# Whole first loads and a re-joined instruction order in a one-core hybrid decoder layer

## The chip, the core and the metric

The kernel runs on one core of a Trainium2 chip. The core has a matrix engine (PE, with PEld for the loading of the stationary operand), a vector engine (DVE), an activation engine (ACT), a general engine (POOL, GpSimd) and a sync engine (SP) whose queue here issues nearly every DMA. Each engine works through its own list of instructions strictly in order; an instruction waits for semaphores of the instructions and transfers it depends on, and everything behind it on that engine waits with it.

The metric is the device time of one execution in microseconds (us); less is better.

## The reference

One decoder layer on a sequence of 512 tokens with 1024 features, batch 1, all in float32. The conditioning vector `c` gives six modulation vectors, the layer mixes tokens by a recurrent group and an attention group, and then runs a squared-ReLU MLP with 4096 hidden features. Cut to what matters here:

```
mod = silu(c) @ ada_w + ada_b
sh1, sc1, g1, sh2, sc2, g2 = split(mod, 6)
h = modulate(rms_norm(x, pre_norm_mix), sh1, sc1)      # h * (1 + sc1) + sh1
z = h @ w_in                                           # first projections
y = concat(rms_norm(gelu(g) * rg_lru(conv4(xr))), rms_norm(nsa_attention(q, k.., v.., gates))) @ w_out
x = x + (1 + g1) * rms_norm(y, post_norm_mix)
h = modulate(rms_norm(x, pre_norm_mlp), sh2, sc2)
y = square(relu(h @ w_ff1)) @ w_ff2                    # up projection, down projection
x = x + (1 + g2) * rms_norm(y, post_norm_mlp)
```

The output must match in float32, so each float32 operand of a large product is split into a high part (`hi`, a rounded form that the matrix engine takes at its fast rate) and a low part (`lo`, the rest), and a product is three matmuls: hi by h, lo by h, hi by the low part of h.

## The kernel before

**Stages.** Tokens lie in four tiles of 128. The kernel loads `x` (`xt[0..3]`, shown by the profile as `r`), sums the squares of each token (`norm_x`, line 864; scratch `att`, totals `stat`), scales `x` by the result, transposes it 128 columns at a time (`tp`), and applies the modulation (`h[j]` and its low part, `pt` being the float32 copy between). `j` runs over eight blocks of 128 features. The loop `first_wave` (line 917) does for each `j`: the modulation sums, the transposes, `h[j]`, the split of the weight tile `a{j}`, and 18 matmuls of 128x512 into six PSUM banks (`f`, `f`, `s`, `s`, `pv`, `pv`). After that come the other projections, the recurrence and the attention, the out projection, the residual, the up projection (`up_first`, `up`, with `up_pair` a seven-product form on tiles B and C made by adding and subtracting raw weight tiles), and the down projection (`down_all`, tiles D, d, e, s, also with fewer products). The end squares and sums the result per token tile and stores.

**Modulation sums.** `silb` is silu(c) spread over all partitions. It is made early: ACT and DVE form `sil`, eight matmuls against `ident` put it into two PSUM banks, and two copies (`silb[0:512]`, `silb[512:1024]`) bring it back. `ada_load` (line 880) loads rows of the modulation weights (`p<-in_ada_a`, two tiles of 128x1024 per `j`, one for the shift, one for the scale). `ada_sums(j)` (line 888) multiplies each tile by `silb` and adds along the row on DVE (`tensor_tensor_reduce`, CUSTOM_DVE_ANT_0 in the profile), giving `sa{j}`, which `h[j]` needs. For `j = 0` alone, tiles 0 and 1 are loaded as two halves each and summed as two halves each.

**Weights.** `Weights.load` (line 536) issues the loads of a tile, `Weights.split` (line 549) makes `hi` and `lo`. Tile `a0` (128x768) is loaded in three pieces of 256 columns and split in three pieces; `a1` to `a7` are loaded and split whole.

**The row of sums for the last gate.** While the up projection ends and the down projection begins, stream G2 (`ada_row`) loads 512 KB tiles `ar<-in_ada_r` and sums them on DVE, eight in turn; each load waits for the buffer of the sum before it.

**What sets the order.** The program first records every instruction as a node (`Clocks.put`, line 291). `flush` (line 283) then emits the nodes sorted by a number that stands for each node in `PLAN`, two characters of base 92 per node. Where an operation can run on more than one engine, the letter in `PLACE` for its stream picks the engine (`a` ACT, `d` DVE, `p` POOL); streams are named, for example `XN` (norm), `WS` (splits), `UP`, `DN` (up and down projection). So PLAN and PLACE together fix, for every engine and for the DMA queue, which instruction comes after which; nothing is decided while the kernel runs. The program has 5468 nodes.

Of the kernel before, what the change touches and what calls it, by code (L numbers as in the profile page):

```python
# [14 lines left out]
P = 128  # L15
S = 512
# [44 lines left out]
    '#0#1#5#=#6#>#8#:#9#2#7#a#H#I#J#K#[#L#M#N#O#Z#$#&###(#)#+#*#,#/#%#.#o#-#p$C#n#G#P#Q#R#S#z#{#|#}#~$#$$'  # L61
    '$%$&$($*$0$1#@#D#E#s#r$8#W#X#l#u#t$7#3#4#B#C#V#F$N#b#Y#k#m#q#v$L#c#e#d#f#h$A$E$)$-$.$/$4$5$6$>$B$D#x'
    '$<#T$:#w$;$H$X$`$U$V$^$_$[$b$i$W$g$e$h$c$j$d$k$f$?#j$@$G$F$+$,$2$3$J$K$R$9$P%4$}%$$y$v$w$|$~%)%#$x%&'
    '%+%;%<%,%%%(%.$S$=$O%2$I$Y$Z$]$a$l$m$p$M$T%8%F%=%@%9%:%C%q%?%B%A%E%K%s%y%D%O%G%N$Q$o$r%3%5$z${%*%-%/'
    '%0%T$n$s%m%t%z%L&&%u%p%w%{%M&(%v%r&/&#%~&*&4%x$t$q%V%7%6%P%Q%R%S%^%]%b%1%W%o&5&-&$&0&I%|&=&.&,&3&V%}'
    '&>&2&1&:&W&G%Y%X%[%>%H%I%J%a%`%e%_%c%n&?&7&;&B&_&Y&@&A&<&D&`&Z&^&X&C&E&b&[%Z%d%h&%&)&+&F&K&M&R&J&P(h'
    '&a&]&h&i&g&e&f(=&m&j&r&o&t(>&n&k&~&u%j%f%i&6&8&9&H&L&O&U&N&T(f&v(?&p&l(@&{&w(I&q&y(D&|&x(N&s&z(F&}#y'
    '(&(6(2(:(#($(((%()(*(u(t,i%k)X(v)^(}(-(3(4(<(5(9(p(|(;(7)*)))Z)i)V)h+&+((o(m+r*X)Y+$*0*1+o*Y&Q(+(0%l'
    '&S(,(1(g(x(l)g)}*V)$*W*#*`*%*a*&*b*v++*w+3*y+5*|+t*},8/i/@/C5U(8.%#A)U(k)S&d(/(A(B(C(j&c(.(i(n(w#;#<'
    '#U#]#^#_#`#g#i$u%U%g(E(G(H)#(r(z)%({*7*]*_*c+1+4-y(J(K(L/(#?/D/n0$(M(O(Q(V(Z([(](^(_(`(a(b(c(d(e*4(s'  # L70
    '(~)(*[+2.J/g(P(R(S(T(U(W(X(Y(q(y)&)+).)/)0)1)6)<)=)W)])|)>)?)@)A)B)C)D)I)T)j)~)J)K)L)N)O)P)Q)R)[)f)k'
    '*$)c)d)e),)-)2)3)4)5)7)8)9):);)E)F)G)H)M)_)`)a)b)l)m)n)o*/*-*5*z)r)s)t)u)v)w)x)y*.*6*x)z){*(*)***+*,'
# [1862 lines left out]
```

## Time and profile before

| what | us |
|---|---|
| median of 3 runs | 588.47 (588.38 to 588.47) |
| the profiled execution's own time | 588.5 |
| its span (first to last instruction) | 586.7 |
| granted TensorE clock, mean | 0.998 of full speed |

The page of the profile gives busy times per engine, a picture of the span in 40 slices, and a chain of work that ended last. The trace behind it answers views: windows (busy time of each engine in a stretch, with counts), the timeline (each instruction with start, duration, and in square brackets how long its engine stood idle before it and what ended that), waits, and the DMA issues. Durations overlap a little on an engine, since instructions are pipelined, so the distance between two starts is the better price where there is one. `L343` is the matmul helper, `L346` the transpose helper, `L353` the ACT helper, `L387` the DVE and POOL helper, `L443` the load: nearly all instructions carry one of these lines and are told apart by their tiles.

### The profile page before, as it was taken

What the parts mean: (1) busy time and instruction counts of PE and PEld (TensorE: products, weight loads), DVE (VectorE), ACT (ScalarE), POOL (GpSimd) and SP (SyncE); (2) the same over time, 40 slices, a digit from 0 to 9 for tenths busy, and PEclk for the clock granted to TensorE, in tenths of its full rate; (3) what the DMA queues carried; (4) which work ended last, traced back from release to release, by engine and by line L of the source; (5) the groups of instructions that cost most, each with busy time, mean ns of one, the idle gap of its engine ahead of it and who ended that gap; (6) DMA issues with size and microseconds to landing.
All of it is one profiled execution on the core that took longest, in us unless ns stands there. A gap on an engine that the chain in (4) does not pass through costs nothing.

```text
span 586.7 us, 9981 instructions
## 1 busy us (share of the span) xinstructions
PE 572.7 (98%) x3410; PEld 499.5 (85%) x3410; DVE 550.1 (94%) x1143; ACT 416.5 (71%) x849; POOL 227.2 (39%) x212
## 2 busy tenths in 40 slices
PE   6999999999999999999999999999999999999995
PEld 5688889878888898899999999998778888788884
DVE  5999999999999999999999999999999999998877
ACT  6658877999999999788747666574757676555314
POOL 4203323656847288651234242532101400114453
PEclk9999999999999999999999999999999999999999
DMA  8989895142242410022342423337343444344303
GB/s 314 417 314 344 295 396 220 59 142 73 94 177 91 151 65 1 19 91 73 109 147 106 139 77 108 110 120 273 129 154 121 157 140 151 122 144 155 132 1 144
DMA packets 27875, 89.12 MB, mean 152 GB/s; under 512 B 3360, under 2 KB 4272, under 8 KB 27824
## 3 DMA queue, kind: packets, MB, share of 16 engines
q1 hardware_dynamic: 27392, 88.27, 42.4%
q8 instruction: 27, 0.44, 0.3%
q10 hardware_dynamic: 432, 0.20, 0.1%
q14 instruction: 24, 0.20, 0.1%
HBM read 86.36 MB, written 2.11 MB: 151 GB/s over the span
## 4 chain that ended last, share of the span: by engine, by line
PE 86%; DVE 7%; issue 1%; ACT 1%; DMA 1%; POOL 0%; DVEq 0%; POOLq 0%
PE f L343 27%; PE pv L343 21%; PE s L343 20%; PE tp L343 14%; PE tp L346 4%; DVE r L387 2%; DVE p L387 2%; DMA ar<-in_ada_r 1%; DVE fT L387 0%; DVE lo_D L387 0%; ACT junk L353 0%; POOL stat L387 0%; DVE K L387 0%; DVE lo_q L387 0%; DVE h L387 0%
## 5 line engine op out<-in xcount | busy, mean ns | idle before, releaser
L387 POOL TENSOR_SCALAR p<-p,den 128x32 f32<-128x32 f32 (+4 forms) x48 | 46.3, 977 | 17.9 <-DVE den L387 10.4
L353 ACT ACTIVATE p<-p,mx 128x32 f32<-128x32 f32 (+4 forms) x96 | 45.2, 474 | 3.9 <-DVE mx L387 3.7
L343 PE MATMUL f<-hi_o,h 128*128 128x512 f32 x128 | 44.5, 406 | 0.0
L353 ACT ACTIVATE fT<-fT 128x512 f32<-128x512 f32 x50 | 29.5, 620 | 9.8 <-DVE fT L387 9.7
L346 PE MATMUL tp<-ident,p 128*128 128x128 f32 x192 | 36.3, 274 | 0.0
L343 PE MATMUL pv<-pt,V 128*128 128x256 f32 x160 | 36.3, 303 | 0.0
L343 PE MATMUL s<-K,Q 128*128 128x288 f32 (+4 forms) x128 | 36.1, 333 | 0.0
L387 DVE TENSOR_TENSOR pt<-tp,pt 128x512 fp32r<-128x512 f32 (+1 forms) x56 | 34.0, 607 | 2.0 <-ACT pt L353 0.5
L353 ACT ACTIVATE hi_B<-raw_A 128x512 fp32r<-128x512 f32 x32 | 20.1, 629 | 19.8 <-DVE raw_A L387 11.6
L387 DVE CUSTOM_DVE_ANT_0 p<-p,silb 128x1024 f32<-128x1024 f32 (+1 forms) x24 | 28.9, 1217 | 0.7 <-DMA p<-in_ada_a 0.7
L343 PEld LDWEIGHTS pv<-pt,V 128*128 128x128 f32 x160 | 26.7, 190 | 3.0 <-DVE pt L387 0.9
L346 PEld LDWEIGHTS tp<-ident,p 128*128 128x128 f32 x192 | 24.4, 141 | 4.8 <-issue 1.3
L343 PEld LDWEIGHTS f<-hi_o,h 128*128 128x128 f32 x128 | 23.5, 188 | 3.6 <-issue 0.3
L353 ACT ACTIVATE pt<-tp 128x512 fp32r<-128x512 f32 (+1 forms) x46 | 24.3, 534 | 3.0 <-PE pv L343 1.6
L353 ACT ACTIVATE junk<-r 128x1024 bf16<-128x1024 f32 (+2 forms) x17 | 13.7, 807 | 16.7 <-DVE r L387 16.2
L343 PEld LDWEIGHTS s<-K,Q 128*128 128x128 f32 x128 | 22.5, 188 | 3.3 <-PE f L343 0.4
L353 ACT ACTIVATE hi_D<-raw_d 128x1024 fp32r<-128x1024 f32 x14 | 14.8, 1060 | 14.1 <-DVE raw_d L387 9.7
L343 PE MATMUL f<-lo_o,h 128*128 128x512 f32 x64 | 24.8, 397 | 0.0
L353 ACT ACTIVATE hi_e<-raw_e 128x1024 fp32r<-128x1024 f32 x13 | 13.7, 1057 | 13.9 <-PE pv L343 5.0
L343 PE MATMUL f<-third,hi_B 128*128 128x256 f32 x96 | 23.4, 284 | 0.0
L387 POOL TENSOR_TENSOR fl<-fS,fh 128x256 fp32r<-128x256 f32 x3 | 6.5, 2176 | 42.6 <-ACT fh L353 42.6
L343 PE MATMUL tp<-r,hi_B 128*128 128x256 f32 x96 | 22.9, 283 | 0.0
(441 smaller groups left out, 2349.8 us busy)
## 6 DMA issues: line engine op xcount, KB each, us to landing
p<-in_ada_t SPq DMA_DIRECT2D x16, 512.0 KB, 7.0
ar<-in_ada_r SPq DMA_DIRECT2D x16, 512.0 KB, 4.3
p<-in_ada_a SPq DMA_DIRECT2D x14, 512.0 KB, 7.2
raw_d<-in_wd SPq DMA_DIRECT2D x14, 512.0 KB, 3.2
raw_e<-in_wd SPq DMA_DIRECT2D x14, 512.0 KB, 3.3
raw_A<-in_wf SPq DMA_DIRECT2D x12, 512.0 KB, 3.2
raw_B<-in_wf SPq DMA_DIRECT2D x12, 512.0 KB, 3.3
r<-in_x SPq DMA_DIRECT2D x8, 512.0 KB, 5.7
```

What stands on the lines that cost most here:

```text
L343: lambda: self.nc.tensor.matmul(out, lhs, rhs, start=start, stop=stop))
L346: self.issue("pe", 0.109, [out], [src], lambda: self.nc.tensor.transpose(out, src, ident))
L353: return "act", cost, lambda: self.nc.scalar.activation(out, src, func, scale=scale, bias=bias, **kw), func
L387: return eng, cost, lambda: fn(out, *args, **kw), None
```

## The change

Four edits. The first three touch code; the program then has 5462 nodes, six fewer (two loads of `a0`, two loads and two sums of the modulation tiles).

1. Tile `a0` is loaded whole, 128x768 in one DMA. Its split stays in three pieces of 256.
2. Modulation tiles 0 and 1 are loaded whole.
3. For `j = 0` each of these tiles is summed by one DVE instruction over 1024 columns, in place of two over 512.
4. PLAN and PLACE are replaced. Apart from the six nodes, old and new lists have the same nodes. From about 68 us to about 297 us of the profiled execution the two orders are the same, instruction by instruction. Before that (first projections, the first seam) and after that (up and down projection, the second seam) the orders differ locally. 82 operations change their engine, nine of them before 68 us.

```
-        cuts = [slice(256 * n, 256 * n + 256) for n in range(3)] if j == 0 else [slice(0, 768)]
-        W.add(f"a{j}", 768, [(lambda r, sl=sl: r[:, sl], inp["wa"][j][:, sl]) for sl in cuts])
+        W.add(f"a{j}", 768, [(lambda r: r[:, :768], inp["wa"][j])])
...
-            for sl in [half(0), half(1)] if k < 2 else [slice(0, 1024)]:
-                load(ada[-1][:, sl], inp["ada_a"][k][:, sl])
+            load(ada[-1], inp["ada_a"][k])
...
-                if j == 0:
-                    part = scol()
-                    dve("tensor_tensor_reduce", w[:, half(0)], w[:, half(0)], silb[:, half(0)], 1.0, first, ALU.mult,
-                        ALU.add, part)
-                    dve("tensor_tensor_reduce", w[:, half(1)], w[:, half(1)], silb[:, half(1)], 1.0, part, ALU.mult,
-                        ALU.add, sa[:, e:e + 1])
-                    continue
                 dve("tensor_tensor_reduce", w, w, silb, 1.0, first, ALU.mult, ALU.add, sa[:, e:e + 1])
...
-PLACE = {'': 'da',
-         'XN': 'aaaaaaaaaaapadapaa',
+PLACE = {'': 'dd',
+         'XN': 'aapaaaaaaadaaaaaaa',
...
-         'UP': 'adadaaddaadpaaaaapddaaaapdaaadapdaaaaappaaaaaddaaaaaddadaaappdaaaapddaaaappaaaaaddaaaaapdaaaaadp'
-          'aaad',
+         'UP': 'adadaadpaadpaaaaadpdaaaappaaaaapdaaaaaddadadaddaaaaapdaaaaapdaaaaaddaaaaadpaaaaaddaaaaappaaaaadd'
+          'aaaa',
```

PLAN is a text that cannot be read by eye. Decoded, its first entries say, queue by queue (brackets are column ranges; `sp` is small work on the recurrence's parameters, `ones` the warm-up matmuls on a constant):

| queue | before | after |
|---|---|---|
| SP loads | x2, x0, a0[256:512], x1, x3, tile 0 first half, tile 1 first half, tile 0 second half, tile 1 second half, tile 3, a0[512:768], a0[0:256], tile 5, tile 2, a1 | x2, x0, x1, x3, tile 0, tile 1, a0, tile 3, tile 5, tile 2, a1 |
| DVE | ident, tab, sil, ctab, cmask, ctab, sp, sp, fold, tab, sp, silb[0:512], five sp, ab, squares of x3, sums: tile 0 and tile 1 first halves, then second halves, sa0 | tab, ctab, tab, ctab, sp, sil, cmask, sp, ident, scale of x2[0:128], sp, fold, three sp, silb[0:512], sp, sp, sp, ab, sp, sp, silb[512:1024], sp, sums: tile 0, tile 1, sa0 |
| ACT | sil, squares of x2, x0, hi_a0[256:512], ..., squares of x1, x3 (half), silb[512:1024], scales of x, h0 | sil, squares of x2, x0, x1, x3 (both halves), scales of x, hi_a0[0:256], hi_a0[512:768], scale of x3, h0 |
| POOL | VC1, totals of squares, scale of x2[128:384], ..., hi_a0[512:768], hi_a0[0:256], clearing of a 128x2048 buffer (`r`) | VC0, K2, clearing of the 128x2048 buffer, totals of squares, scale of x0[128:384], ..., hi_a0[256:512] |
| PE | one warm-up, eight silb matmuls, fourteen warm-ups, transposes of x | four warm-ups, eight silb matmuls, one transpose, eight warm-ups, transposes of x, six warm-ups |

Behind `sa0`, DVE's old list has: sum of tile 3, lo_a0 in three pieces with the sum of tile 5 and the low part of h0 after them, sum of tile 2, sa1. The new list has: lo_a0 in three pieces, sums of tiles 3 and 5, the low part of h0, sum of tile 2, sa1.

In the second seam 73 operations change engine, all in splits, relu, squares, and the additions of the up and down projection. Between 400 and 430 us of the profiled execution four go from POOL to DVE and none the other way: a 256-column `fT`, a 512-column `r`, a 256-column `fS` and a 512-column `fl`. Between 430 and 500 us two go from POOL to DVE (a 256-column `fl`, a 256-column `fS`) and one from DVE to POOL (a 256-column `fS`). Between 500 and 550 us thirteen leave DVE and nine come to it. The order of the weight tiles through the matrix engine stays as it was (single matmuls move by at most 54 places); the order in which the DVE's additions, the `lo` splits and the eight sums of G2 follow each other changes locally.

More of the change, by code (lines that the diff above doesn't have):

```diff
@@ new lines @@
+    '$/$0#F#N#O#`#P$5#H#Q#R#_#]#^#/#0#L#M#W#[$I#S#T#U#V#m#v$6#k#l#n$B$A$$$%$($*$2$3$4$=$@$C#s$8#t$:#u$9$D'
+    '$Q$^$M$T$O$X$`$_$N$W$P$Y$b$c$a$]$[$Z$>$;$?$F$E#w$&$)$1$G$H$h$7$K%0$v$r$w$x$q$s$y$u%)%<%$$t%#$|%5%@%%'
+    '${$L$<$J%.%-$R$S$U$V$d$f$n$e$j%4%8%9%6%B%&%=%:%A%7%G%D%E%K%F%H%p%r%N$l$i$k%1%/$z$}$~%(%*%+%V$g$m%i%L'
+    '%n%I%q%u%O%w%o%s%t%v%P%x%}%z&#%{&&$p$o%T%3%2%C%J%Q%R%[%]%a%,%S%l%y%~&$&+&*&(%|&N&K&7&,&G&-&O&L&8&1&H'
+    '%Y%U%W%;%>%?%M%^%`%e%_%b%k&.&R&M&P&2&U&6&W&V&Q&3&Z&J&]&X&S&I&[%d%Z%c&/&0&9&:&;&<&A&=&C(d&b&^&Y&j&T&i'
@@ new lines @@
+    '&c(9&_&k&f&n&q(:&d&l&{&r%g%f%h&%&)&4&5&@&?&F&>&D(b&s(;&e&m(<&x&t(E&o&v(@&y&u(J&p&w(B&z#K(#(3(/(6&|&}'
+    '($&~(%(&(q(p,c%j)R(r)W(x(*(0(1(8(2(5(l(w(7(4)$)#)T)c)P)b*|*}(k(i+l*R)S*z***++i*S&E(((-%m&h()(.(c(t(h'
+    ')a)w*P({*Q)y*Y){*Z)|*[*p+$*q+-*s+/*v+n*w,2/c/:/=5O#I-{&g#J(g)N&a(,(=(>(?(f&`(+(e(j(s#5#8#G#X#Z#a#c#d'
+    '#e#g#h%X(A(C(D(z(n(v(|&B*1*V*X*]+++.-s(F(G(H.}#j/>/h/z(I(K(M(R(V(W(X(Y(Z([(](^(_(`(a*.(o(y(~*U+,.D/a'
+    '(L(N(O(P(Q(S(T(U(m(u(})%)))*)+),)1)7)8)Q)V)v)9):);)<)=)>)?)D)O)d)x)E)F)G)I)J)K)L)M)U)`)e)z)])^)_)&)('
@@ new lines @@
+    ')-).)/)0)2)3)4)5)6)@)A)B)C)H)X)Y)Z)[)f)g)h)i*)*&*/*t)l)m)n)o)p)q)r)s*(*0*r)t)u)})~*#*$*%*4*-*W*u*5*6'
+    '*7*8*9*:*;*<+#+0,a*2*3*>*?*@*A*B*D*E*L*M*N*O*a*b*c*d*e*i*j*k*l*m*n*~*{+&+%+R+p,e*=*C*F*G*H*I*J*K*^+T'
+    '+o,`*_*`*y*f*h+5)j)k+S*,+h*T+1+2+3+4+N+M+g+m+6+7+8+9+:+;+<+>+?+@+A+B+C+D+E+F+G+H+I+J+L+P,-,1,b+K+V+W'
+    '+X+Y+Z+[+]+`+a+b+q+s+t+u+v+w+x+y+z+{+|+}+~,+-n.w0Z-:-x.A.~+r,5,7,3-<-v/4,8,9,:-;-t.?/?,<,=,A,D,E,F,G'
+    ',H,I,K,L,M,N,O,P,Q,R,T,_,n,],f*g*o+(,,+)+O+*+Q+^+_+k,(+f,*+j,),g,i,o-*-(,j-),l,k,;,>,?,@,B,C,U,V,W,X'
@@ new lines @@
+    ',r,s,t,u,w,x,z,{,|,},~-$-%-&-I-r-+-B-3-4-5-6-8-9-U-X-Z+=+U+c,^+d,&+e,%-[-]-^,#,$,0,Z,/,Y,.,[,m-=-A-N'
+    '-O-F-D-C-P-_-`-a-b-d-e-f-g-h-i-j-k-m-y-l/@-#-/-1-2-E-R-0-7-L-u.).*.1.2.3.4.6.E.F.n/90[,J,S,q-M,p-G.G'
+    '.H.I,4,6,h-,.L.S.T.U.V.W/2/|0_.X.Y.Z.d.e.f.s.|.t/;/f/v0]/7-S-c.&.+.-.7.;.N.{-~.#.$.%.<.B...0.>.O---.'
+    '->-K-?-H,v,y-@-J-Q-w.x-z-|.:.=-}.R.].^._.`/)/Z/{/g-T-Y-p.o-o.q-V-W-q.9.g.h.i.k.v/#.[.a.j.l/0/<.(.,.C'
+    '.r.M.u./.5.@.p.y/3/]0./_/R/^/Y/N/O/P/Q///A/e/i/p/q/r/s.J.K.Q/U.P/S.b.c.z/10$0%0-1*04/k/l/m/n/w/x0&0('
@@ new lines @@
+    '0)0*0305.m/$/5/X/6/T/%/./8/V/`/b/d0W/t0O0X0,0?0D0I0J0C0E0T0U0K0M0c0i/~0+/K/W0l0p0{1+1-0m0n0r0s0z1)0d'
+    '0f0g0q1&1(0#0//j/u1:1A1B1C161718191T2#1J1d1e1g1@1D2,25070N2S2T2X2Y2Z2]2b3Z36/L/[1/141.120V/}1P1N0Q0R'
+    '02000y0x0P.8/&/(011L2c1M/*/+/,1W0Y1>0S/-/D/E0a1U1S1Q1R1s2^1X1}/F/G/H1Y1n1m1~2{2x/I/J092>0:0;0<0=0>0@'
+    '2D0A0B0L0`0b3|1V/B/C/M/o06080F0G0H0e0h0j0k0o0t0u0v0w0|0}0~1#1$1%111013151,1?3}1l1t1u1v1w1x1z1|202122'
+    '2E2F2G2H2I2N2O2P2U2g2i2k2l2u2v3Y4]1G1]2$2-1r2*1;1<1=2)1E1F1K1Z1[1^1_1`1a1c1h1i1j1k2L1y1{2%2.2&2/1H1I'
@@ L179 @@
           'dpadadadadadadddaddadddaddadddaddadddaddadddaddadddaddadddaddadddaddadddaddadddaddadddaddadddadd'
-          'adddaddadddaddadaddapaddadaddadaddadaddddaddapaddadaddadaddadaddapaddadadddddddapaddadapadaddp',
+          'adddaddadddaddadaddapaddadadpadaddadaddadaddadaddapaddadaddadaddadaddapadpapaddadadpdpadddddad',
          'AW': 'aaaaaaaapdppadadppppadad',
```

205 lines of the change are left out of this document (90 added, 115 removed).

## Prediction

> **What bounds the kernel now.** I read the page first, then the windows, then the chain that ended last.
>
> ```profile
> PE 572.7 (98%) x3410; PEld 499.5 (85%) x3410; DVE 550.1 (94%) x1143; ACT 416.5 (71%) x849; POOL 227.2 (39%) x212
> ...
> PE 86%; DVE 7%; issue 1%; ACT 1%; DMA 1%; POOL 0%; DVEq 0%; POOLq 0%
> ```
>
> ```profile
> core 0: us, PE busy (x) PEld busy (x) DVE busy (x) ACT busy (x) POOL busy (x), PEclk, DMA share, GB/s
> 0.00:12.00 12.00, 7.96 (x50) 7.43 (x50) 6.12 (x22) 8.15 (x20) 6.34 (x18) 1.00 0.84 293
> 12.00:24.00 12.00, 10.05 (x45) 6.97 (x46) 11.54 (x26) 8.24 (x13) 4.74 (x4) 1.00 1.03 418
> 24.00:36.00 12.00, 12.00 (x61) 9.71 (x60) 12.00 (x25) 6.89 (x10) 0.00 (x0) 1.00 1.03 415
> ...
> 350.00:400.00 50.00, 50.00 (x412) 49.38 (x411) 48.24 (x95) 31.72 (x55) 17.57 (x16) 1.00 0.37 131
> 400.00:430.00 30.00, 29.76 (x132) 23.39 (x131) 28.70 (x45) 17.69 (x30) 6.68 (x5) 1.00 0.55 175
> 430.00:500.00 70.00, 69.98 (x309) 57.62 (x308) 68.92 (x104) 48.14 (x78) 10.00 (x3) 1.00 0.45 148
> 500.00:550.00 50.00, 50.00 (x219) 40.64 (x219) 47.38 (x74) 25.91 (x42) 12.77 (x9) 1.00 0.39 127
> ```
>
> One row from the chain shows what a matmul costs when nothing is late:
>
> ```profile
> 515.18 1.36 PE tp L343 x6
> ```
>
> That is 0.227 us from one 128x512 matmul to the next. In 500 to 550 us, 219 matmuls at 0.227 make 49.7 of 50 us; in 430 to 500 us, 309 make 70.1 of 70. PE runs there without a gap, and no reordering can win more than a few tenths. The room is in the first 24 us, where PE is busy 18 of 24 and part of that is warm-up, and at 400 to 430 us. Everything from 24 us on is carried along by what time the first projections get going: a lead won there arrives at the end, as long as DVE, busy 94%, keeps it.
>
> **The change part by part: the opening.** The timeline of the start, in order of time:
>
> ```profile
> 1.42 0.24 DVE L387 TENSOR_SCALAR ident<-p 128x128 f32<-128x128 f32 x1 [1.42 <-POOL p L705]
> ...
> 4.47 0.17 DVE L387 SCALAR_TENSOR_TENSOR sil<-sil,vecs 128x8 f32<-128x8 f32 x1 [2.39 <-ACT sil L353]
> ...
> 4.69 3.60 PE L343 MATMUL tp<-ident,sil 128*128 128x128 f32 x16 [2.30 <-DVE sil L387]
> ...
> 5.95 0.17 DVE L387 TENSOR_SCALAR sp<-vecs 128x4 f32<-128x4 f32 x1 [0.84 <-DMA vecs<-in_vecs]
> ...
> 8.12 3.29 PE L343 MATMUL s<-ones 128*128 128x128 f32 x28
> ...
> 9.95 0.75 DVE L387 CUSTOM_DVE_ANT_0 p<-p,silb,vecs 128x512 f32<-128x512 f32 x1 [0.15 <-DMA p<-in_ada_a]
> ...
> 11.42 0.70 DVE L387 CUSTOM_DVE_ANT_0 p<-p,silb 128x512 f32<-128x512 f32 x1 [0.71 <-DMA p<-in_ada_a]
> ...
> 13.67 0.22 DVE L387 SCALAR_TENSOR_TENSOR sa<-sa,ab,vecs 128x1 f32<-128x1 f32 x1
> ...
> 14.36 2.37 POOL L387 TENSOR_SCALAR hi_a<-raw_a 128x256 fp32r<-128x256 f32 x2 [1.69 <-DMA raw_a<-in_wa]
> ...
> 15.05 0.73 PE L343 MATMUL s<-h,hi_a 128*128 128x512 f32 x2 [1.34 <-ACT h L353]
> ...
> 15.94 0.61 DVE L387 TENSOR_TENSOR lo_a<-raw_a,hi_a 128x256 fp32r<-128x256 f32 x1 [0.22 <-POOL hi_a L387]
> 16.67 1.81 POOL L429 MEMSET r<- 128x2048 f32 x1
> ...
> 17.10 1.22 DVE L387 CUSTOM_DVE_ANT_0 p<-p,silb 128x1024 f32<-128x1024 f32 x1
> ...
> 18.24 0.69 DVE L387 TENSOR_TENSOR h<-pt,h 128x512 fp32r<-128x512 f32 x1
> ...
> 20.05 0.35 DVE L387 SCALAR_TENSOR_TENSOR sa<-sa,ab,vecs 128x1 f32<-128x1 f32 x2
> ...
> 21.20 0.50 PE L343 MATMUL s<-h,hi_a 128*128 128x512 f32 x1
> ```
>
> What the reader is to see: the first sums at 9.95 and 11.42 wait for their tiles (0.15 and 0.71 us idle), `sa0` is ready at 13.9, `h0` lets PE begin at 15.05, and `sa1` at 20.3 (the 20.05 row holds `sa1`, 0.22 us, and `sa2`) lets the second block begin at 21.20. Between the last two sums DVE is the chain.
>
> *The loads.* The same 5.5 MB go through the queue to tile `a1`; four fewer starts. The new queue puts x (4 x 512 KB), tiles 0 and 1 (512 KB each) and `a0` (384 KB) first: 3.54 MB, while the first window moved 293 GB/s x 12 us = 3.52 MB. So `a0` is whole at about 12.0 us, tile 1 earlier by 0.39 MB at 418 GB/s, 0.94 us, at 11.1, and tile 0 by another 1.25 us at 9.8. Before, `a0`'s last pieces came at about 14.3 (the 14.36 row). That frees its split by over 2 us.
>
> *The wait that is added.* The new DVE list puts `sp`, which needs the second vector load, ahead of `sil`, and `ident` ninth. That load ended a wait at 5.95 (before, `sil` waited for nothing of it). Behind it stand `sil`, `cmask`, `sp` and then `ident`; an operation of 0.17 us keeps the engine for 0.09, since neighbours overlap by 0.08 (17.10 to 18.24 is 1.14 for a row of 1.22), so `ident` is done at about 5.95 + 0.17 + 3 x 0.09 + 0.24 = 6.6 in place of 1.66, and the eight silb matmuls begin at about 6.65 in place of 4.69. They take the row's 3.60 us and end at 10.25. The copy of the second half of `silb`, now on DVE (0.69 us, by the 512-column row at 18.24), runs from about 10.5 to 11.15. So whole sums start at about 11.2, though tile 0 has been there since 9.8: the wait for the tile has become a wait for `silb`. Two whole sums, 1.14 us each from start to start, and `sa0` make 2.5 us: `sa0` at 13.7 to 13.9, just where it was. By this, edits 1 to 3 alone give nothing up to `sa0`.
>
> The Trainium skill ("TensorE: Matmul & The Clock Gate", section "Part 1: The HAM clock gate") says that the array starts at half rate and is released after about 3.4 us of sustained activity, counted in time, not matmuls. By that rule the slow stretch moves along with the group and 10.25 stands; the 3.60 us row, then 28 instructions in 3.29 us, agrees in size, while the granted clock of the first window, 1.00, doesn't show it.
>
> If on the contrary the slow rate (3.60/16 = 0.225 us each, then 3.29/28 = 0.118) is tied to the time since the start, the change of rate stays at about 8.1: six or seven instructions are slow, the rest take 0.118, and the group ends at about 9.2. The sums then follow their tiles: `sa0` at about 12.6. That is a rival below.
>
> *Behind `sa0`.* Before, DVE needed 20.27 - 13.89 = 6.38 us to `sa1`, with 0.22 us idle for POOL's `hi_a` before one `lo_a0` and the rest out of step. After, `hi_a0` comes from ACT and POOL before `sa0`, and DVE has only the work: three `lo_a0` (3 x 0.53 by the 0.61 row less the overlap), three sums of 1.14 to 1.2, 0.61 for the low part of `h0`, 0.22 for `sa1`: 5.9 us. So `sa1` comes 0.5 us earlier, and the second block of PE starts at about 20.7. PE has the slack for it: its 18 matmuls of 0.227 from 15.05 need 4.1 us, some 4.6 with four transposes. The cleared buffer (1.81 us of POOL) moves into POOL's idle start (6.34 busy of 12), where the next it has to do needs ACT's squares first.
>
> From 24 us PE and DVE are both full (12.00 of 12 us). DVE must hold its lead: four half sums of 0.70 to 0.75 (2.9) become two whole ones of 1.22 (2.4), a square of half a tile goes to ACT and a `silb` copy of the same size comes, so it has 0.5 us less to do. So I take **-0.5 us** from the opening, between 0 and -1.5.
>
> **The change part by part: up and down projection.**
>
> ```profile
> 418.86 3.29 DMA ar<-in_ada_r
> ...
> 424.82 1.14 DVE lo_D L387
> 426.55 1.15 DVE lo_D L387
> ```
>
> ```profile
> 401.90 2.33 DVE L387 TENSOR_TENSOR lo_f<-raw_f,hi_f 128x1024 fp32r<-128x1024 f32 x1 [0.27 <-issue]
> ...
> 406.15 1.22 DVE L387 TENSOR_TENSOR lo_f<-raw_f,hi_f 128x1024 fp32r<-128x1024 f32 x1
> ...
> 416.51 2.31 DVE L387 CUSTOM_DVE_ANT_0 ar<-ar,silb,ab 128x1024 f32<-128x1024 f32 x1
> ...
> 419.36 0.75 DVE L387 TENSOR_TENSOR fl<-fS,fh 128x256 fp32r<-128x256 f32 x2
> 420.03 0.68 DVE L387 TENSOR_TENSOR fl<-fT,fh 128x512 fp32r<-128x512 f32 x1
> ...
> 422.17 1.28 DVE L387 CUSTOM_DVE_ANT_0 ar<-ar,silb,ab 128x1024 f32<-128x1024 f32 x1 [0.53 <-DMA ar<-in_ada_r]
> ```
>
> ```profile
> 401.87 1.29 POOL L387 TENSOR_TENSOR r<-fT,r 128x512 fp32r<-128x512 f32 x1
> ...
> 416.21 1.53 POOL L387 TENSOR_TENSOR fl<-fT,fh 128x512 fp32r<-128x512 f32 x1 [0.17 <-ACT fh L353]
> ```
>
> ```profile
>   DVE lo_D L387: 1.3, 3
> ...
>   ACT hi_D L353: 0.7, 2
> ```
>
> The last fence is from the idle time of PE's matmuls and weight loads between 297 and 570 us and what ended it; its longest row is 1.3 us, three times, for `lo_D`. The chain shows where: a G2 sum waits 0.53 us for its load, and the two `lo_D` behind it come late at 424 to 428. In the new order the work that stands between that sum and the one before is longer by about a microsecond, so the 0.53 goes; of the 1.3 I expect some 0.4 back, because another thing happens at the same place: four operations come from POOL, two of 0.68 (512 columns) and two of 0.38 (256; the row of two says 0.75), together 2.1 us, where DVE has 30 - 28.70 = 1.3 us left. Against it stands what POOL costs DVE: the same `lo_f` took 2.33 us beside a POOL operation and 1.22 without, the same G2 sum 2.31 and 1.28; 2.1 us that come back if those operations leave POOL. So the price lies between +2.1 and 0; I take 0.1, near the end that these two pairs of rows show.
>
> At 430 to 500 us two 256-column operations come and one goes, net 0.4 against 1.1 us of DVE idle time: nothing, and at most 0.4. At 500 to 550 DVE is relieved, but PE had no gap there: nothing gained. Before 400 us PE is gap-free too (412 matmuls in 50 us, no idle). SP's order of some weight tiles is swapped, while the windows show DMA at a share of 0.37 to 0.55 and 127 to 175 GB/s, against 418 in the opening: nothing. The tail keeps its order on PE: nothing.
>
> Sum: -0.5 (opening) - 0.4 (lo_D) + 0.1 (POOL's work on DVE) = -0.8. The profiled execution took 588.5, 0.03 over the median of 588.47. **588.5 - 0.8 = 587.7 us**, inside the 0.2% (1.18 us) that a measurement of this kernel can tell from no change.
>
> **The rivals.**
>
> *The opening gives more (faster).* If the silb group speeds up at 8.1 as before, `sa0` comes at 12.6 and the chain behind it, still 5.9 us, ends 1.7 earlier than in the profile; tile 2, with tiles 3 and 5 ahead of it 1.57 MB behind `a0`, lands 3.8 us after 12.0 at 418 GB/s, at 15.8, before its sum. PE's own 4.6 us from `h0` at 14.6 (hi_a0 and scales on ACT before it) end at 19.2, so the lead is about 1.5. With half to all of the 1.3 us for `lo_D`: 588.5 - 1.5 - 0.9 = **586.1 to 586.7**. For it: the tiles are there in time. Against: the row of 3.60 us starts from an idle engine, and the group again does.
>
> *No lead survives (no change).* Whole loads do nothing because `silb` is the wait, and if `ident` slips by another 0.3 us (each small operation at its 0.17 in place of 0.1), `sa0` slips with it to 14.1 and takes the 0.5 away. The change then doesn't do what it says: **588.3**.
>
> *DVE becomes the bound at 400 to 430 (slower).* If the four operations slow nothing less by leaving POOL (if 2.33 and 2.31 have another cause, or other POOL work moves there), DVE has 2.1 us more with 1.3 us idle that consists of waits for `ar` and `hi_D`, so can't be filled. The G2 loads behind it shift too, and `lo_D` comes 2.1 us later, all of it on PE, which then waits in the row that shows 1.3 now. 588.5 - 0.5 + 2.1 = **590.1**; it decides once more than 1.6 of the 2.1 us relief fails to come, the opening giving no more than 0.5 (1.6 - 0.5 is about 0.2%). Against it: two pairs of rows with the same excess.
>
> **How the numbers follow.** Forecast 0.36, opening gives more 0.34, no lead 0.14, DVE bound 0.16. Faster by over 0.2% means under 587.3, slower over 589.65. The first rival is faster; of the forecast's own spread (587.0 to 588.4) a little falls under 587.3: faster 0.38. The slower rival gives 0.14, with its mild end (half the relief lost, 589.05) still within the bound. Same: 0.48. The range for 8 in 10 reaches over most of the fast rival and to the mild end of the slow one: 586.1 to 589.4. The forecast's own range is 587.0 to 588.4.
>
> **What would show it.** In the timeline after: the silb matmuls start near 6.65 and the first whole sum near 11.2, its idle time ended by PE or `silb` and not by a DMA; `a0` lands near 12.0; `sa0` near 13.8; the second block's first matmul near 20.7. A sum at 10 would show the first rival. In the chain, the pair of `lo_D` rows and the `ar` load at 418 to 428 are shorter or gone, and `lo_f` and the G2 sums take 1.2 to 1.3 us each; `lo_D` waits of over 2 us in the idle time of PE would show the slower one. I'm wrong if PE has gaps at 430 to 570 us that it doesn't have now, or if the lead of the second block is not still there at 60 us.

## The result, and the profile after

| | us | ratio to the kernel before (95% interval) |
|---|---|---|
| before, median of 6 runs | 588.47 (588.38 to 588.58) | |
| after, median of 6 runs | 584.11 (583.34 to 584.80) | 0.9926 (0.9913 to 0.9939) |
| after, profiled execution | 583.79, span 581.7 | |
| after once more, beside 11 other runs of the kernel before (median 588.48), 6 runs | 584.34 (583.70 to 586.81) | 0.9938 (0.9925 to 0.9952) |

The change makes the kernel 4.4 us faster (0.61 to 0.87%). The forecast was 587.7, a gain of 0.8, with a range from 586.1 to 589.4: wrong, since the gain was five times as large. Where the time went is read from the same views as before. The windows of the changed kernel first:

```profile
core 0: us, PE busy (x) PEld busy (x) DVE busy (x) ACT busy (x) POOL busy (x), PEclk, DMA share, GB/s
0.00:12.00 12.00, 7.67 (x43) 7.07 (x44) 7.89 (x24) 8.70 (x22) 8.85 (x21) 1.00 0.87 335
12.00:24.00 12.00, 10.93 (x59) 8.63 (x59) 11.96 (x25) 9.61 (x17) 1.24 (x2) 1.00 1.03 419
350.00:400.00 50.00, 50.00 (x411) 49.55 (x410) 48.41 (x94) 33.51 (x59) 15.10 (x13) 1.00 0.39 132
400.00:430.00 30.00, 30.00 (x133) 24.35 (x133) 29.00 (x50) 19.59 (x35) 0.87 (x2) 1.00 0.57 186
430.00:500.00 70.00, 70.00 (x310) 57.93 (x310) 69.13 (x110) 45.98 (x74) 4.32 (x4) 1.00 0.41 136
500.00:550.00 50.00, 50.00 (x223) 41.39 (x222) 45.83 (x67) 29.90 (x48) 14.48 (x9) 1.00 0.47 157
```

In the opening PE does more by 24 us (18.6 us busy in place of 18.0). In 500 to 550 us it has 223 matmuls in place of 219, though "busy" reads 50.00 both times. A count in a window is good to one or two matmuls at its edges; by the starts of the matmuls, as worked out below, the change gains 0.56 us in this stretch, and the column of busy time never showed them as missing. Between 400 and 430 us POOL works 0.87 us in place of 6.68.

The second view is the list of what ended the idle time of PE's matmuls and weight loads (L343) in the up and down projection: how many us in total, and how many times. The prediction showed two rows of it; these are the others of the kernel before, from 297 to 570 us:

```profile
  DVE lo_e L387: 0.8, 3
...
  DVE fT L387: 0.6, 2
  POOL lo_s L387: 0.4, 1
  ACT last L353: 0.3, 1
```

and this is the whole list of the kernel after, for the same work (292 to 565 us):

```profile
  ACT last L353: 0.4, 2
  ACT hi_D L353: 0.2, 1
```

Before, the six rows sum to 4.1 us; after, to 0.6. The list points at the right places, but it is no measure of PE's loss. Nearly all of it is idle time of the weight loads; the matmuls alone have 0.2 us of it, one wait for `lo_D`. It also leaves out waits under about 0.15 us, and the transpose of `row`, which stands on another line.

The timeline of the opening after:

```profile
5.74 0.17 DVE L387 TENSOR_SCALAR sp<-vecs 128x4 f32<-128x4 f32 x1 [0.52 <-DMA vecs<-in_vecs]
...
6.33 3.39 PE L343 MATMUL tp<-ident,sil 128*128 128x128 f32 x16 [2.66 <-DVE ident L387]
...
11.07 1.29 DVE L387 CUSTOM_DVE_ANT_0 p<-p,silb,vecs 128x1024 f32<-128x1024 f32 x1
...
13.74 0.22 DVE L387 SCALAR_TENSOR_TENSOR sa<-sa,ab,vecs 128x1 f32<-128x1 f32 x1
...
13.88 1.09 DVE L387 TENSOR_TENSOR lo_a<-raw_a,hi_a 128x256 fp32r<-128x256 f32 x3
...
18.98 0.35 DVE L387 SCALAR_TENSOR_TENSOR sa<-sa,ab,vecs 128x1 f32<-128x1 f32 x2
...
20.13 0.50 PE L343 MATMUL pv<-h,hi_a 128*128 128x512 f32 x1
```

The silb group waits for `ident` until 6.33, the first sum starts at 11.07 without a wait for its tile, `sa0` is where it was (13.74, before 13.67), and the second block starts at 20.13, 1.07 us earlier than in the first trace of before.

To see where time comes from, I took from two traces the start of the n-th matmul in each; the difference is PE's **lead** over the kernel before at that point. A stretch in which the lead does not change is one where both kernels are equally fast. All leads below are worked out in this way, against the profiled execution of before (span 586.7).

| run | second block starts at | lead gained 295 to 395 us | 395 to 436 us | 436 us to the last matmul |
|---|---|---|---|---|
| before | 21.20 | | | |
| after | 20.13 | 1.22 | 1.19 | 1.16 |
| before, another execution | 20.77 | 0.02 | -0.04 | -0.01 |
| after, another execution | 20.39 | 1.20 | 1.16 | 0.95 |

The three stretches of after make 3.57 us, the larger part of the result. The lead grows in small steps, each where the kernel before has a wait. Before 395 us there are six waits that stretch the distance between two matmuls by 0.17 to 0.32 us each, 1.2 us in all; only one of them, 0.27 us of a weight load for `fT` at 331.79, is long enough for the list above. In the next stretch they are 0.39 us at 408 to 413 us (`hi_D` and `last`) and 0.85 us at 423 to 429 us (`row` and two `lo_D`). Behind it they are 0.32 us at 472 to 476 us (`hi_D`), 0.41 us at 500 to 505 us (`fT` and `lo_e`), 0.11 us at 530 to 536 us (`lo_e`) and 0.27 us at 555 to 560 us (`lo_s`), in the times of the kernel before. That the list shrinks by about as much as the lead grows is partly chance.

### The profile page after: what moved, and what is told of

It is laid out like the page before. It is cut to its first block, busy times and chain, and to the rows that moved or that the text cites. A ratio compares the mean times of both kernels' runs of the same rounds, so it can differ in the third digit from the quotient of the medians.

```text
span 581.7 us, 9966 instructions
## 1 busy us (share of the span) xinstructions
PE 569.0 (98%) x3410; PEld 500.2 (86%) x3410; DVE 547.9 (94%) x1138; ACT 421.9 (73%) x860; POOL 206.4 (35%) x202
## 4 chain that ended last, share of the span: by engine, by line
PE 88%; DVE 5%; ACT 3%; issue 1%; DMA 1%; POOL 1%; SPq 0%; DVEq 0%; ACTq 0%; POOLq 0%
PE f L343 29%; PE pv L343 21%; PE s L343 20%; PE tp L343 14%; PE tp L346 4%; DVE r L387 3%; DMA r<-in_x 1%; ACT r L353 1%; POOL stat L387 1%; ACT p L353 1%; ACT junk L353 1%; DVE p L387 0%; ACT L353 0%; DVE ar L387 0%; DVE h L387 0%
## 5 line engine op out<-in xcount | busy, mean ns | idle before, releaser
L387 POOL TENSOR_SCALAR p<-p,den 128x32 f32<-128x32 f32 (+4 forms) x48 | 47.1, 994 | 17.9 <-DVE den L387 10.4
L353 ACT ACTIVATE p<-p,mx 128x32 f32<-128x32 f32 (+4 forms) x96 | 45.2, 473 | 3.4 <-DVE mx L387 3.2
L343 PE MATMUL f<-hi_o,h 128*128 128x512 f32 x128 | 44.5, 406 | 0.0
L343 PE MATMUL s<-K,Q 128*128 128x288 f32 (+4 forms) x128 | 36.2, 334 | 0.2 <-DVE mx L387 0.2
L346 PE MATMUL tp<-ident,p 128*128 128x128 f32 x192 | 36.3, 274 | 0.0
L343 PE MATMUL pv<-pt,V 128*128 128x256 f32 x160 | 36.3, 303 | 0.0
L387 DVE TENSOR_TENSOR pt<-tp,pt 128x512 fp32r<-128x512 f32 (+1 forms) x56 | 34.0, 607 | 1.9 <-ACT pt L353 0.7
L387 POOL TENSOR_TENSOR lo_e<-t,hi_e 128x512 fp32r<-128x512 f32 x1 | 1.3, 1300 | 94.8 <-ACT hi_e L353 94.8
L353 ACT ACTIVATE hi_B<-raw_A 128x512 fp32r<-128x512 f32 x34 | 21.4, 629 | 17.3 <-DVE raw_A L387 14.9
L353 ACT ACTIVATE fT<-fT 128x512 f32<-128x512 f32 x50 | 29.6, 619 | 5.2 <-DVE fT L387 5.1
L387 DVE CUSTOM_DVE_ANT_0 p<-p,silb 128x1024 f32<-128x1024 f32 x24 | 29.6, 1249 | 0.0
L343 PEld LDWEIGHTS pv<-pt,V 128*128 128x128 f32 x160 | 26.7, 190 | 3.0 <-DVE pt L387 0.9
L346 PEld LDWEIGHTS tp<-ident,p 128*128 128x128 f32 x192 | 24.4, 141 | 4.7 <-issue 1.4
L353 ACT ACTIVATE hi_D<-raw_d 128x1024 fp32r<-128x1024 f32 x14 | 14.8, 1060 | 18.0 <-DVE raw_d L387 11.0
L353 ACT ACTIVATE pt<-tp 128x512 fp32r<-128x512 f32 (+1 forms) x46 | 24.3, 535 | 3.0 <-PE pv L343 1.6
L343 PEld LDWEIGHTS f<-hi_o,h 128*128 128x128 f32 x128 | 23.5, 188 | 3.5 <-issue 0.3
L343 PEld LDWEIGHTS s<-K,Q 128*128 128x128 f32 x128 | 22.5, 188 | 3.9 <-DVE mx L387 0.5
L343 PE MATMUL f<-lo_o,h 128*128 128x512 f32 x64 | 24.8, 397 | 0.0
L353 ACT ACTIVATE junk<-r 128x1024 bf16<-128x1024 f32 (+2 forms) x17 | 13.7, 807 | 15.1 <-DVE r L387 14.7
L343 PE MATMUL f<-third,hi_B 128*128 128x256 f32 x96 | 23.1, 282 | 0.0
L387 DVE TENSOR_TENSOR lo_B<-raw_A,hi_B 128x512 fp32r<-128x512 f32 x29 | 20.3, 698 | 1.7 <-ACT hi_B L353 1.2
L343 PE MATMUL tp<-r,hi_B 128*128 128x256 f32 x96 | 21.7, 282 | 0.0
```

Source lines behind the costliest of these rows:

```text
L343: lambda: self.nc.tensor.matmul(out, lhs, rhs, start=start, stop=stop))
L346: self.issue("pe", 0.109, [out], [src], lambda: self.nc.tensor.transpose(out, src, ident))
L353: return "act", cost, lambda: self.nc.scalar.activation(out, src, func, scale=scale, bias=bias, **kw), func
L387: return eng, cost, lambda: fn(out, *args, **kw), None
```

## The experiments

Runs 1, 2, 3 and 8 were taken together on one chip, runs 5, 6, 7 and 9 together on another, and 4, 10, 11 and 12 on that second chip later; each group has its own runs of the kernel before beside it (medians 589.03, 588.90 and 588.48). The kernels of the runs are some lines shorter: L336, L339, L346 and L380 there are the matmul, transpose, ACT and DVE helpers that stood at L343, L346, L353 and L387. Where an edit is one of order or engine letters, it is shown as what changes in the decoded lists. Most texts below speak of the stretch "where both orders agree": about 68 to 297 us.

**1. The new opening alone.**

```
 code edits 1 to 3, new order and letters up to the common stretch
-new order and letters behind it
+old order and letters behind it
```

> The code edits and the new order up to the stretch where both orders agree; from there the old order and the old engine letters. Theory (the two seams add up): second block's first matmul near 20.1 us as in the changed kernel, PE's lead over the kernel before about 1.1 us at 24 us and still 1.0 to 1.1 at 297 us, the stalls of 0.07 to 0.34 us between 297 and 550 us all there as before; time 587.3 to 587.5. Rival (the lead of the opening is what lets the DVE keep ahead later): the lead grows behind 297 us to 2 us or more; time 585 to 586.5.

Measured 587.29 us, ratio 0.9970 (0.9956 to 0.9984). The second block starts at 20.39, and from 295 us on the lead grows by nothing (-0.03, then 0.10, then -0.29). The seams do not help each other: the opening does not lift the later stages. Its list of PE's idle time still holds the old rows:

```profile
  ACT hi_D L346: 1.6, 4
  DVE lo_D L380: 1.3, 3
  DVE lo_e L380: 0.6, 3
```

**2. The new second seam alone.**

```
 old code, old order and letters up to the common stretch
-old order and letters behind it
+new order and letters behind it
```

> The old code and old order up to the stretch where both orders agree, from there the new order and the new engine letters. Theory (the two seams add up): no lead up to 297 us, then about 1.2 us gained by 400 us, 1.2 more by 436 us, 0.9 more by 520 us; time 584.8 to 585.3. Rival (the second seam needs the lead of the opening): under half of it, 586.5 to 588.

Measured 585.48 us, ratio 0.9943 (0.9925 to 0.9962). The lead gained is 1.40, 1.19 and 1.18 us in the three stretches, as much as in the whole change, and the list of PE's idle time is down to two rows:

```profile
  ACT last L346: 0.4, 2
  DVE lo_C L380: 0.2, 1
```

So the second seam carries about 3.4 to 3.8 us by itself and needs nothing from the opening. The two seams add, within the intervals: 0.30% and 0.57% make 0.87%, against 0.74% and 0.62% measured for both.

The trace of this run also shows the old opening a second time: its second block starts at 20.55, and in the repeat of before (run 12) at 20.77, where the one trace I had shows 21.20. The new opening gives 20.13, 20.39, 20.39 and 20.33 in four traces (after, run 1, run 11, run 5; runs 6 and 7 have 20.42 and 20.27). The mean moves from 20.84 to 20.31: at the second block the opening is worth about **0.5 us**, and the 1.07 of a single pair of traces was partly luck. By time it is worth more: the interval of run 1 is 0.9 to 2.6 us. At 60 us the six traces with the new opening are 0.7 us ahead of the three with the old one (mean leads 1.02 and 0.30); where the rest of run 1's time comes from is not shown.

**3. The whole loads and sums alone.**

```
-            for sl in [half(0), half(1)] if k < 2 else [slice(0, 1024)]:
-                load(ada[-1][:, sl], inp["ada_a"][k][:, sl])
+            load(ada[-1], inp["ada_a"][k])
...
-                if j == 0:
-                    part = scol()
...
-                    continue
```

> The kernel before with modulation tiles 0 and 1 loaded whole and summed whole, nothing else: a0 still in three pieces, old order and engines. Theory (the order, not the whole loads, makes the opening's lead): sa0 moves from 13.67 to somewhere in 13.0 to 13.7, the second block's first matmul by at most 0.3 us, time 588.2 to 588.5. Rival (the whole loads make it): second block near 20.3, time 587.4 to 587.6.

Measured 588.95 us, ratio 0.9996 (0.9984 to 1.0009): no change to be seen. Its trace is a bad one for the opening, since PE ran slow in it:

```profile
10.00:20.00 10.00, 8.10 (x49) 6.65 (x48) 8.33 (x19) 6.00 (x12) 8.06 (x7) 0.85 1.03 414
```

The granted clock was 0.85 from 10 to 20 us, where those of before, after and runs 1, 2, 8 and 12 have 1.00, so the trace says nothing on the second block. The time is clouded by the same thing: five of the ten executions have a mean granted clock of 0.994 or 0.995 (589.05 to 589.81 us), and none of the 16 runs of the kernel before beside them is under 0.996. The other five have a median of 588.40, 0.6 us under the kernel before. So `sa0` came a microsecond early, at 12.65, and no gain shows in the median; whether the whole sums would be worth a few tenths at the full clock, this run does not settle.

**4. The new order with loads in pieces.**

```
-SP:  ..., tile 0, tile 1, a0, ...
+SP:  ..., tile 0 in two halves, tile 1 in two halves, a0 in three pieces, ...
-DVE: ..., sum of tile 0, sum of tile 1, sa0
+DVE: ..., sums of two halves, sums of two halves, sa0
```

> The changed kernel's order and engine letters, but a0 loaded in three pieces and modulation tiles 0 and 1 loaded and summed as halves, each piece right behind the other. Theory (the new order makes the opening's lead, the whole loads only spare small change): DVE has two more sums, 0.5 us; landings of a1 and tiles behind 0.3 to 1 us later; second block's first matmul 0.3 to 0.7 us later than in the changed kernel, time 0.2 to 0.7 us above it. Rival (the whole loads make the lead): second block at 21 or later, time 1.0 us or more above it.

Measured 584.91 us, ratio 0.9939 (0.9926 to 0.9952), beside 584.34 and 0.9938 for the changed kernel on the same chip. The second block starts at 20.67, 0.28 later than in the changed kernel beside it. The whole loads, the part of the change that gives it its name, are worth 0.3 us of its trace and less than the runs can tell; the order makes the rest.

**5. Four operations back on POOL.**

```
-DVE: fT (256 columns), r (512), fS (256), fl (512) between 400 and 430 us
+POOL: the same four, at the same places of the order
```

> The changed kernel with four operations of 400 to 430 us given back to POOL by their engine letters (one fT, r, fS and fl each), all else the same. Theory (a POOL operation beside it stretches a DVE operation by about 1.1 us): two or three DVE operations at 400 to 420 us take 2.0 to 2.4 in place of 1.2 to 1.3 us, the lo_D behind them come 0.5 to 1 us late and PE waits for them again, lead lost there 0.4 to 1.0 us; time 0.4 to 1.0 us above the changed kernel. Rival (the order of the G2 sums alone removed the lo_D stall): no PE idle time for lo_D, time within 0.2 us of the changed kernel.

Measured 585.66 us, ratio 0.9947 (0.9932 to 0.9962). In the stretch from 395 to 436 us the lead shrinks by 0.23 in place of growing by 1.19. The stretch before keeps its gain (1.22); the one behind gains 0.57, where the changed kernel gained 1.16 and 0.95 in its two traces. By time alone the loss is not proved, since this interval overlaps both of those in the table of the result. The timeline of DVE and of POOL in this run:

```profile
396.41 2.31 DVE L380 CUSTOM_DVE_ANT_0 ar<-ar,silb,ab 128x1024 f32<-128x1024 f32 x1
...
412.53 2.31 DVE L380 CUSTOM_DVE_ANT_0 ar<-ar,silb,ab 128x1024 f32<-128x1024 f32 x1
...
415.65 1.22 DVE L380 TENSOR_TENSOR raw_D<-raw_D,raw_d 128x512 f32<-128x512 f32 x1
416.79 1.23 DVE L380 TENSOR_TENSOR fl<-fT,fh 128x512 fp32r<-128x512 f32 x1
```

```profile
395.75 1.89 POOL L380 TENSOR_TENSOR r<-fT,r 128x512 fp32r<-128x512 f32 x1 [1.48 <-ACT r L346]
...
412.16 1.60 POOL L380 TENSOR_TENSOR fl<-fT,fh 128x512 fp32r<-128x512 f32 x1 [11.93 <-ACT fh L346]
```

Two G2 sums take 2.31 us each, beside POOL operations that start 0.4 to 0.7 us before them; two 512-column operations take 1.22 and 1.23 in place of 0.68. In the changed kernel the same two sums and those between them take 1.3:

```profile
396.78 1.27 DVE L387 CUSTOM_DVE_ANT_0 ar<-ar,silb,ab 128x1024 f32<-128x1024 f32 x1
...
412.19 1.28 DVE L387 CUSTOM_DVE_ANT_0 ar<-ar,silb,ab 128x1024 f32<-128x1024 f32 x1
```

These four rows alone cost DVE 2 x 1.03 + 2 x 0.54 = 3.1 us, more than the 2.1 us for which the four operations would run on DVE. PE pays for it at one place, the transpose of the `row` that the G2 sums build:

```profile
424.31 0.27 PE L339 MATMUL tp<-ident,row 128*8 128x128 f32 x1 [1.21 <-DVE row L380]
```

In the changed kernel the same transpose, at 423.33, waits for nothing. The distance from the start before it to its own is 1.61 us in place of 0.23, so this one wait is nearly all of the 1.4 us of lead lost. The mechanism of the theory holds; the lead lost was more than the 0.4 to 1.0 expected, and the place was wrong, since PE waited for `row`, and behind that wait hardly for `lo_D` (0.2 us). The list of idle time has two more rows that the changed kernel has not, at 450 and 489 us, in the stretch behind:

```profile
  ACT fh L346: 0.4, 1
  DVE fl L380: 0.4, 1
```

**6 and 7. Order without letters, letters without order.**

```
 run 6: new order everywhere; behind the common stretch the old engine letters
 run 7: new opening; behind the common stretch the old order, with the new engine letters
```

> The changed kernel's order everywhere, but from the stretch where both orders agree the old engine letters. Theory (order and letters are both needed, since each list is fitted to its own engines): PE's lead grows behind 297 us by 1 to 2 us in place of 3.5. Rival (the order makes it, the letters hardly matter): grows by 3 us or more. Second rival (the letters make it): by less than 0.7 us.

> The opening as in the changed kernel; from the stretch where both orders agree the old order with the new engine letters. Theory (both are needed): lead grows behind 297 us by 0.5 to 2 us. Rival (order makes it): by less than 0.7 us or it shrinks. Second rival (letters make it): by 3 us or more.

Measured 611.20 us (ratio 1.0382, 1.0364 to 1.0400) and 620.32 us (1.0561, 1.0516 to 1.0605). No theory foresaw it: all expected some gain but one rival of run 7, which allowed for a shrinking lead. Both are far slower than either kernel. PE waits mostly for DVE's splits, in the first run at 300 to 350 us already, where it has 356 matmuls (before, 414 in the same stretch) and the granted clock is 0.93:

```profile
300.00:350.00 50.00, 46.96 (x356) 45.58 (x357) 43.73 (x81) 25.89 (x47) 14.34 (x12) 0.93 0.25 85
```

The list of idle time says for what in the second:

```profile
  DVE lo_e L380: 22.2, 10
```

An order that is written out in full is fitted to its engine letters: an operation that goes to another engine stands there behind work that was not meant to be ahead of it. The 3.5 us of the second seam are a property of the pair.

**8. `ident` and `sil` first.**

```
-DVE: tab, ctab, tab, ctab, sp, sil, cmask, sp, ident, ...
+DVE: ident, tab, sil, ctab, ctab, tab, sp, cmask, sp, ...
```

> The changed kernel with ident first on DVE and sil ahead of the two ctab/tab operations and of the operation that waits for the second vector load. Theory (silb is what the first sums wait for in the changed kernel): silb matmuls start at 4.9 to 5.1 in place of 6.33, silb is whole near 9.6, the first sum starts at the landing of tile 0 (about 9.7), the second at about 10.9, sa0 near 12.3 in place of 13.74, second block's first matmul near 19.2; 0.7 to 1.1 us less than the changed kernel, about 583.2. Rival (ACT, busy with scales and hi_a0 until 13.1, becomes the gate of h0): sa0 early but second block only 0.2 to 0.4 earlier, about 583.8.

Measured 584.83 us, ratio 0.9936 (0.9913 to 0.9959): not better than the change. The silb group starts at 5.07 and `sa0` comes at 12.70, as expected, but `sa1` at 19.26 and the second block at 20.57. POOL's timeline shows why:

```profile
10.30 2.43 POOL L380 TENSOR_SCALAR stat<-stat 128x1 f32<-128x1 f32 x1
12.82 0.56 POOL L380 TENSOR_TENSOR stat<-stat,nhalf 128x1 f32<-128x1 f32 x1
```

A POOL operation on one column took 2.43 us, until the two whole sums that DVE had begun at 10.22 were through; in the changed kernel it ran at 9.97, ahead of the sums, in 0.35. With it the scale of x3, `hi_a0` and `lo_a0` came late. The late `silb` of the changed kernel, which I had called a wait, was what let POOL finish. (The profiled execution is the slowest of the four, 586.77 us, by two losses of 1.1 us each at 489 and 527 us; nothing of that lies in the opening.)

**9 and 10. Two steps further.**

```
 run 9, besides run 8:
-ACT: squares of x3, first half, second half;  POOL: scale of x0[128:384], ..., totals of x3
+DVE: squares of x3, second half;  ACT: first half, scale of x0[128:384];  POOL: totals of x3
 run 10, besides run 9:
-PE: silb group, one transpose, eight warm-ups, six transposes
+PE: silb group, eight warm-ups, one transpose, six transposes
```

> As ident_first, and besides half the squares of x3 on DVE in place of ACT, and the scale of x0[128:384] on ACT in place of POOL, so that POOL's totals of x3 are done before the first whole sum starts. Theory (in ident_first the lead was lost because POOL's total of x3 took 2.43 us beside two whole sums on DVE): the totals take 0.3 and 0.57 us, sa0 at 12.7 to 13.0, hi_a0 before sa0, second block's first matmul at 19.2 to 19.6, about 1 us ahead of the 20.4 of the run with the new opening alone; time 0.7 to 1.1 us below ident_first. Rival (the loads of the tiles behind, or ACT, hold the second block): second block at 20.0 to 20.5, time as ident_first.

> As ident_first2, and besides eight warm-up matmuls moved from behind the first transpose to right behind the silb group on PE. Theory (in ident_first2 sa1 was 0.7 us earlier, but PE had begun its first block no earlier, since warm-ups at the slow rate, 3.62 us for 16, stood in its queue ahead of the transposes that h0 needs): the 16 follow the silb group without a gap and take 1.9 to 2.0 us, transposes done by 12.5, first main matmul at 14.4 to 14.7, second block at 19.5 to 19.8; 0.5 to 0.9 us below the changed kernel on the same chip. Rival (something else holds PE, ACT's scales or h0): first main matmul at 15.2 or later, second block 20.1 or later, time as the changed kernel.

Run 9 measured 584.74 us, ratio 0.9922 (0.9900 to 0.9944). POOL's totals took 0.33 and 0.56, `sa1` came at 18.50, 0.76 before run 8, but PE began its first block only at 15.67 and the second at 20.35. The timeline of PE:

```profile
9.71 0.48 PE L339 MATMUL tp<-ident,r 128*128 128x128 f32 x1 [1.16 <-ACT r L346]
9.98 3.62 PE L336 MATMUL s<-ones 128*128 128x128 f32 x16
13.40 1.07 PE L339 MATMUL tp<-ident,r 128*128 128x128 f32 x6
```

PE idled 1.16 us behind the silb group, the warm-ups behind that gap ran at 0.226 us each, and the transposes that `h0` needs stood behind them. Run 9 thus ended where its rival had put it, at run 8's time. In run 10 the warm-ups follow the silb group directly:

```profile
4.68 3.41 PE L336 MATMUL tp<-ident,sil 128*128 128x128 f32 x16 [1.01 <-DVE sil L380]
7.93 1.95 PE L336 MATMUL s<-ones 128*128 128x128 f32 x16
...
14.53 0.47 PE L336 MATMUL s<-h,hi_a 128*128 128x512 f32 x1 [0.60 <-ACT h L346]
```

Run 10 measured 583.77 us, ratio 0.9919 (0.9907 to 0.9932); the changed kernel beside it (run 11) 584.34, 0.9938 (0.9925 to 0.9952). Its second block starts at 19.44, 0.95 before run 11 (0.69 before the first trace of the changed kernel), and that lead is there to the end (5.54 us over before, 4.72 in run 11). The expected 0.5 to 0.9 us is there in the trace; the two intervals overlap, so by time alone it is not proved that run 10 beats the change.

**11 and 12. The two kernels once more.**

> The changed kernel once more, as the measure on this chip for the run beside it and for how far runs of one order lie apart. All theories: 4.0 to 4.7 us under the kernel before.

> The kernel before once more, for a trace from this chip. All theories: time within 0.2% of the runs of the kernel before, and the same places where PE waits: 0.2 to 0.4 us each for lo_D at 424 to 428 us.

Run 11: 584.34 us, 4.1 under the runs beside it. Run 12: 590.01 us, 0.26% over, a little out of what was expected, and it shows where single executions differ: its lead falls from 0.45 to -1.39 at one matmul, 76.71, and stays there.

```profile
74.84 1.06 ACT L346 ACTIVATE hi_x<-raw_x 128x1024 fp32r<-128x1024 f32 x1 [2.03 <-DVE s L380]
...
76.71 0.66 PE L336 MATMUL s<-fold,pt 128*128 128x64 f32 x4 [1.67 <-ACT pt L346]
```

Other single jumps are 1.1 us at 489 us in runs 8 and 9, again 1.1 us at 527 us in run 8, and 0.8 us near 68 us. The last is in all four traces of runs 1, 2, 3 and 8, with the old opening and the new, and in none of the ten other traces: it goes with that chip or that session and not with an order. What starts the jumps was not tried. At 424 to 428 us run 12 loses what before loses: the lead doesn't change there.

## Why the prediction was wrong, point by point

**Where PE can still gain: the step that failed.** "PE runs there without a gap, and no reordering can win more than a few tenths", and, behind it, "PE had no gap there: nothing gained". I had multiplied 219 by 0.227, got 49.7 of 50, and called the difference nothing. It was real: by the starts the change gains 0.56 us in that stretch, and such waits of 0.1 to 0.5 us, most of them in the weight loads, lie all over the up and down projection. I quoted the longest row of the list of idle time and dismissed the rest. Runs 1 and 2 show what it was worth: the second seam gave about 3.5 us where the forecast had -0.4 and +0.1. The stretches that I priced at nothing (before 395 us, after 436 us) gave 1.2 us each. Which of the 73 engine changes and of the moves in the order ended which of these small waits was not tried, except for the four of run 5.

**`lo_D` at 418 to 428 us: right place, wrong size.** The chain of the changed kernel has neither the `ar` load nor the two `lo_D` any more:

```profile
399.28 10.92 PE f L343 x48
...
414.33 3.17 PE f L343 x14
417.74 3.17 PE f L343 x14
```

From 423 to 429 us 0.85 us of lead came back, not 0.4, the wait for `row` beside the two `lo_D` included; another 0.39 came from `hi_D` and `last` at 408 to 413 us, for which I had no term.

**The four operations from POOL: the sign was wrong.** I bounded their price between 0 and +2.1 us and took 0.1. By run 5 it is a gain: leaving them on POOL costs 1.4 us of lead. The two pairs of rows that I had (2.33 and 1.22, 2.31 and 1.28) were the right ones; I set their 2.1 us against 2.1 us of added work and stopped at zero, though in run 5 POOL slows more DVE operations than the two in my rows. It does not slow all: beside a POOL operation at 399.48 DVE's 256-column additions, which read one operand from a PSUM bank (`s`, `pv`, `tp`), keep their 0.41 us. That also settles the slower rival: nothing of it came.

**The opening: right in steps and, at the second block, in size.** The silb group was forecast for 6.65 and came at 6.33; the first sum for 11.2 (11.07), `sa0` for 13.8 (13.74), the second block for 20.7 (20.13 to 20.39). The gain at the second block is 0.5 us by the means, as forecast; the time of run 1 says more, and that stays open. `a0` was there at 11.84 (forecast 12.0). That the wait for the tile turned into a wait for `silb` is in the trace. The step behind `sa0` was priced at 5.9 us and took 5.24 (13.74 to 18.98): three `lo_a0` follow each other in 1.09 us in the trace, where I had 1.6 from a row that ran beside POOL.

**The rule on PE's clock: the fixed time fell, the moving stretch is not sure either.** The group started 1.64 us later and kept its length (3.39 us, before 3.60), so the rival in which the rate changes at about 8.1 us fell. But how long PE stays slow behind the group's start differs between two executions of one order. In after the sixteen warm-ups behind the group and one transpose take 1.95 us; in run 11, again without a gap, 3.02:

```profile
9.80 1.95 PE L343 MATMUL s<-ones 128*128 128x128 f32 x16
```

```profile
6.60 3.78 PE L336 MATMUL tp<-ident,sil 128*128 128x128 f32 x16 [2.93 <-DVE ident L380]
...
10.39 3.02 PE L336 MATMUL s<-ones 128*128 128x128 f32 x16
```

In run 11 ten of these sixteen still start 0.213 us apart and the last ones 0.112, so the rate changed near 12.6 us, 6 us behind the group's start; in after it changed near 9.2, less than 3 us behind it. The Trainium skill ("TensorE: Matmul & The Clock Gate", section "Part 1: The HAM clock gate") names about 3.4 us of sustained activity. Before, after and run 10 are near that (the rate changes 3.3, 2.8 and 2.9 us behind the group's start); run 11 is not, and the measurement decides. Runs 9 and 10 don't settle it: 16 instructions directly behind the group take 1.95 us in run 10 and 3.62 behind a gap of 1.16 us in run 9, but run 11 was slow without a gap. The granted clock of the 0 to 12 us window reads 1.00 in all of these.

**The first rival.** It had the right direction for the wrong reason: 586.1 to 586.7 from an opening with 1.5 us, still 2 us over what was measured. In run 8 `sa0` did come at 12.70 and the second block did not follow: the mechanism of the rival was not enough, POOL's totals and PE's warm-ups stood in the way.

## What to carry to other kernels

On an engine that is 98% busy, look at every small wait of a stage, those of the weight loads too, before calling it full; waits of 0.1 to 0.3 us can make more than the one that stands out, and a busy column of 100% doesn't show them. What they cost is read from the starts of the same matmuls in two traces, better than from a sum of idle rows. An order and its choice of engines are one thing: neither half of a tuned pair was worth anything without the other. Where a reordering moves a start forward, look what had used the wait, on the other engines too.

## What I had not expected of the hardware

In these rows DVE and POOL hold each other up in both directions. POOL's clearing of two buffers held DVE's small operations in the changed kernel: the `ctab` operation took 0.22 us before.

```profile
2.04 2.85 DVE L387 TENSOR_SCALAR ctab<-p 128x128 f32<-128x128 f32 x1 [0.18 <-POOL p L720]
2.19 2.71 DVE L387 TENSOR_TENSOR tab<-tab,p 128x512 f32<-128x512 f32 x1
```

```profile
2.10 0.97 POOL L429 MEMSET K<- 64x1056 f32 x1
3.02 1.80 POOL L429 MEMSET r<- 128x2048 f32 x1
```

Both DVE operations end at 4.9, just behind the clearing (4.82), and runs 1, 5 and 11 show the same 2.85 us; in run 8, where `ctab` starts at 4.93 behind the clearing, it takes 0.22 again. In run 8 it is POOL that stands still for 2.43 us behind two sums on DVE. And the time at which PE's matmuls change from 0.213 to 0.112 us each moved by 3.4 us between two executions of one order.
